# A chunked RWKV-7 chain of two products a chunk instead of three: the inverse times the keys and times the value terms is made once per group

## The chip, the cores and the metric

The kernel runs on one core of one Trainium2 chip. The metric is the device time of one execution, in microseconds (us). The core has five engines that run side by side, each with its own row of instructions taken in order: TensorE (PE, matrix products into PSUM), VectorE (DVE), ScalarE (ACT), GpSimd (POOL), and SyncE (SP), which here issues all DMA transfers. They wait for one another through semaphores.

## The reference

One decoder block on x (1 x 2048 x 1024), float32. After RMSNorm and an adaLN modulation, a single product with `w_in` gives the inputs of two token mixers and of their gates; a causal convolution branch and an RWKV-7 branch follow, are gated, projected and summed, and an output projection, the residual and a last RMSNorm close the block. The part that the change touches is the RWKV-7 recurrence of 16 heads of 64 channels:

```python
def step(state, inp):
    r_t, w_t, k_t, v_t, kk_t, b_t = inp
    sk = jnp.einsum('bhvk,bhk->bhv', state, kk_t)
    state = (state * w_t[:, :, None, :] - sk[..., None] * b_t[:, :, None, :]
             + v_t[..., None] * k_t[:, :, None, :])
    return state, jnp.einsum('bhvk,bhk->bhv', state, r_t)
...
kk = (k * k_k).astype(f32).reshape(hd)
kk = kk / jnp.maximum(jnp.sqrt(jnp.sum(kk * kk, axis=-1, keepdims=True)), L2_EPS)
...
o = _rwkv7_scan(r, decay.reshape(hd), k, v, kk, kk * a)
```

## The kernel before

**Tiling.** Four blocks of 512 tokens. In each block the input projection makes 73 tiles of 128 output channels x 512 tokens. Every such product is made of f32r matmuls of split operands (`h_hi,w_hi`, `h_lo,w_hi`, `h_hi,w_lo`), eight k-steps of three matmuls each, in the PSUM tile `ps_main`. These f32r rows are the bulk of PE's work. Each block has four groups of two pairs; a pair is two heads, 128 channels. Tokens are cut into chunks of 64, eight per block.

**The pair** (`pair`, line 720) prepares operands: decays `E1`, `E2`; `KR` (keys and receptances times decays) and `BK`; the products KR·BK masked into `As` (four quarters per chunk, the triangle to be inverted among them); `tk`, the transpose of BK; values `uv`. The squared norms `sq` are summed by eight matmuls with N=2 per pair into `rn`, which stays as a factor: it multiplies the triangles (`As<-As,rn`, two steps per pair) and, later, each chunk's solution.

**The group** (`group`, line 870) inverts 32 unit triangles of 64x64 (two pairs, two heads, eight chunks): the 32x32 diagonal parts on POOL over 31 steps (`La`, `TT`, reached by DMA through DRAM), the off-diagonal parts by 32x32 matmuls `lower` and `upper`. Then comes the chain over eight chunks with the state `S`, three products a chunk that each wait for the one before through DVE:

1. `xo<-S,KR` (state times keys); DVE adds the value term and writes `Xz`;
2. `xo<-Xz,As` (times the inverse; the next chunk's value term `xval` is interleaved, `xo<-uv,As`); DVE multiplies by `rn` and writes `uv`;
3. `xo<-uv,tk` (state increment, four products of one head each); four DVE steps write `S`.

After every second chunk eight more `xo<-uv,As` products give the outputs (`olast`). Behind the chain, outputs are normalised, transposed (`late<-ident,uv`), gated and stored.

**What sets the order.** In the first phase the program order is written by generators (`Task`) that a planner advances: `note` (line 85) keeps a modelled clock for each engine, and after each k-step (three f32r rows) tasks whose operands are ready on that clock may put their instructions, a burst, into the rows. `burst` lets a task wait up to `JOIN` for another burst while a chain runs. The order is fixed when the program is built; on the chip each engine takes its row in order. In the second phase (`pout`, `pmean`) a scheduler orders the rows. Every instruction is recorded at the helper's line 127, so names of tiles tell the places apart: `out<-in`.

Of the kernel before, what the change touches and what calls it, by code (L numbers as in the profile page):

```python
# [13 lines left out]
ALU = mybir.AluOpType  # L14
# [37 lines left out]
SEM, SWITCH, JOIN = 0.1, 0.14, 2.0  # L52
# [19 lines left out]
def hybrid_block(ctx: ExitStack, tc: tile.TileContext, x, vecs, convk, w2a2, final_g, ada, w_in, w_co, w_ro, w_o, crow, out,  # L72
# [436 lines left out]
    hones = bones.bitcast(F32)[:, 0::64]  # L509

    Xz = c1.tile([P, 2, 2, P], F32, name="Xz")
    nc.gpsimd.memset(Xz, 0.0)
# [207 lines left out]
    def pair(G, q_, box):  # L720
        b, pr, uv, Asb, rn = G.b, 2 * G.g + q_, G.uv, G.As[q_], G.rn
# [50 lines left out]
        pss = pa.tile([P, NCH // 2, 2], F32, name="aux", tag="aux")  # L772
# [30 lines left out]
        rlo = e1.tile([P, TB], F32R, name="s_lo", tag="s_lo")  # L803
# [16 lines left out]
        for e in range(2):  # L820
            sl = prow(e)
            tri = Asb[sl, :, e::2, kcol(e)]
            ENT[TRE].tensor_tensor(out=tri, in0=tri, in1=rq[sl].rearrange("p c h -> p h c").unsqueeze(3).broadcast_to(
                [64, 2, NCH // 2, CH]), op=ALU.mult)
# [31 lines left out]
    def opened(b, g, h, lora):  # L856
        G = Group()
        G.b, G.g, G.h, G.lora, G.tri, G.pairs, G.chained, G.gated, G.normed = b, g, h, lora, 0, 0, False, False, False
        G.uv = l3.tile([P, NCH, 2, P], F32, name="uv", tag="uv", bufs=2)
        for e in range(2):  # L860
            nc.gpsimd.memset(G.uv[prow(e), e::2], 0.0)
        G.As = [l3.tile([P, 2, NCH, P], F32, name="As", tag="As", bufs=ASB) for _ in range(2)]
        G.R = [{}, {}]
        G.rn = lt.tile([P, 2, NCH // 2, 2], F32, name="rn", tag="rn")
        return G
# [4 lines left out]
    def group(G, before):  # L870
        g, b, As, uv, rn, R = G.g, G.b, G.As, G.uv, G.rn, G.R
# [18 lines left out]
        nc.gpsimd.memset(TTf[0:64, 0::34], 1.0)  # L890
        nc.gpsimd.memset(TTf[64:128, 1::34], 1.0)
# [37 lines left out]
        yield both(ok(T11), free, bank("late"), bank("aux", 2))  # L929
# [16 lines left out]

        turns(lower)
# [4 lines left out]
        yield ok(Qs)  # L952

        turns(upper)
        with tc.high_priority(HP):
            for e in range(2):
                lo_, hi_ = quarters(e)
                for q in range(2):
                    nc.vector.tensor_copy(As[q][lo_, :, e::2, hi_], pq[e][lo_, q])
        locked[0] = False  # L960
        yield ok(*As)

        O = uv[:, 0::2]
        Sg = S[g]
# [3 lines left out]

        def xval(c, n):

            q, hh, hs = every[3 - n]
            nc.tensor.matmul(xo[c % 2][prow(c % 2), 2 + q, hs], As[q][:, hh, c, kcol(c % 2)], uv[:, c, q, hs],
                             start=(n == 0), stop=(n == 3), skip_group_check=True)

        def xcopy(c):
            nc.scalar.copy(Xz[prow(c % 2), c % 2], xo[c % 2][prow(c % 2), 2:4])

        def olast(c):
            for n, (q, hh, hs) in enumerate(every):
                for e in range(2):  # L980
                    nc.tensor.matmul(xo[e][vrow(e), q, hs], As[q][:, hh, c + e, rcol(e)], uv[:, c + e, q, hs],
                                     start=False, stop=(n == 3), skip_group_check=True)
            with tc.high_priority(HP):
                for e in range(2):
                    nc.scalar.copy(O[vrow(e), c // 2], xo[e][vrow(e), 0:2])

        yield bank("xo", 2)
        for n in range(4):
            xval(0, n)
        with tc.high_priority(HP):  # L990
            xcopy(0)
        for c in range(NCH):
            cc, e = c // 2, c % 2
            pr_, b_ = prow(e), xo[e]
            es = slice(e * 128, e * 128 + 128)
            Se = lt.tile([P, 2, P], F32, name="Se", tag="Se", bufs=1)
            for q in range(2):
                nc.tensor.matmul(b_[:, q, :], R[q]["KR"][:, cc, es], Sg[:, q, :], start=(q == 0), stop=False,
                                 skip_group_check=True)
            with tc.high_priority(HP):  # L1000
                for q in range(2):
                    nc.scalar.mul(Se[:, q, :], Sg[:, q, :], R[q]["pe"][:, c:c + 1])
                nc.vector.tensor_tensor(out=Xz[pr_, e], in0=b_[pr_, 0:2], in1=Xz[pr_, e], op=ALU.add)
            yield ok(Xz)

            for n, (q, hh, hs) in enumerate(every):
                nc.tensor.matmul(b_[pr_, q, hs], As[q][:, hh, c, kcol(e)], Xz[:, e, q, hs],
                                 start=(n == 0), stop=(n == 3), skip_group_check=True)
                if c + 1 < NCH:
                    xval(c + 1, n)  # L1010
            with tc.high_priority(HP):
                if c + 1 < NCH:
                    xcopy(c + 1)
                nc.vector.tensor_tensor(out=uv[pr_, c].rearrange("p q (h n) -> p q h n", n=64),
                                        in0=b_[pr_, 0:2].rearrange("p q (h n) -> p q h n", n=64),
                                        in1=rn[pr_, :, cc, :].unsqueeze(3).broadcast_to([64, 2, 2, 64]), op=ALU.mult)
            yield ok(uv)
            for q, hh, hs in every:
                nc.tensor.matmul(b_[hs, 2 + q, 0:64], R[q]["tk"][:, c, hs], uv[:, c, q, hs], start=False,
                                 stop=(q + hh == 2), skip_group_check=True)  # L1020
            with tc.high_priority(HP):
                for q, hh, hs in every:
                    nc.vector.scalar_tensor_tensor(out=Sg[hs, q, hs], in0=b_[hs, 2 + q, 0:64],
                                                   scalar=R[q]["pe"][hs, c:c + 1], in1=Se[hs, q, hs],
                                                   op0=ALU.mult, op1=ALU.add)
            yield ok(Sg)
            if e:
                olast(c - 1)
                yield ok(uv)
# [69 lines left out]
    def conv(b, h, j):  # L1099
# [21 lines left out]
        evac(value(project(h, ("in", T_VAL + j)), convs[-2:-1]))  # L1121
# [92 lines left out]
    def lora_split(ps, out_):  # L1214
        yield hx.room(3)
        lf, ll, lx = hx.take("lora"), hx.take("lora_lo"), hx.take("lora_x")
        yield from shifted(ps, T_LORA, lambda: lf)
        yield ok(lf)
# [439 lines left out]
```

## Time and profile before

| | |
|---|---|
| median of 3 runs | 2994.11 us (2994.05 to 2997.04) |
| profiled execution | 2994.35 us, span 2992.6 us |
| mean granted TensorE clock | 0.973 |
| ACT, POOL busy | 1064.4 us (36%), 1273.2 us (43%) |
| DMA | 680.02 MB, mean 227 GB/s |

A row of the timeline gives start, duration, engine, operation, and in brackets the idle time before it with what ended it. A row of the waits gives for whom an engine waited: total us, times, longest. A row of the groups gives busy us and mean ns of one. Matmuls are pipelined, so a recorded duration is longer than the distance to the next start; an f32 matmul leaves two records, a transpose or an f32r matmul one. The slices of the page show where PE is less than full: at the start, and otherwise in tenths:

```profile
PE   5999899989899999799999998999999997899998
DVE  6787787868677878685778686858597836543433
POOL 2464646532516565436356654354654624100000
```

The first phase ends near 2498 us (slice 34), and the output projection follows.

### The profile page before, as it was taken

What the parts mean: (1) busy time and instruction counts of PE and PEld (TensorE: products, weight loads), DVE (VectorE), ACT (ScalarE), POOL (GpSimd) and SP (SyncE); (2) the same over time, 40 slices, a digit from 0 to 9 for tenths busy, and PEclk for the clock granted to TensorE, in tenths of its full rate; (3) what the DMA queues carried; (4) which work ended last, traced back from release to release, by engine and by line L of the source; (5) the groups of instructions that cost most, each with busy time, mean ns of one, the idle gap of its engine ahead of it and who ended that gap; (6) DMA issues with size and microseconds to landing.
All of it is one profiled execution on the core that took longest, in us unless ns stands there. A gap on an engine that the chain in (4) does not pass through costs nothing. (4 is left out here: it accounts for less than half of the span.)

```text
span 2992.6 us, 51518 instructions
## 1 busy us (share of the span) xinstructions
PE 2793.2 (93%) x19152; PEld 2220.9 (74%) x19152; DVE 2055.5 (69%) x3671; ACT 1064.4 (36%) x2168; POOL 1273.2 (43%) x1793
## 2 busy tenths in 40 slices
PE   5999899989899999799999998999999997899998
PEld 4777777767677777577777775877777776788988
DVE  6787787868677878685778686858597836543433
ACT  4544343434233434333433344323334323221211
POOL 2464646532516565436356654354654624100000
PEclk9999999999999999899999998999999998999999
DMA  7785857666658576677677665765656857776665
GB/s 286 268 288 199 279 204 266 213 225 218 214 172 295 178 252 212 226 250 231 197 236 239 204 235 176 252 233 184 231 203 192 269 164 268 263 234 224 211 225 176
DMA packets 359051, 680.02 MB, mean 227 GB/s; under 512 B 131536, under 2 KB 150288, under 8 KB 358800
## 3 DMA queue, kind: packets, MB, share of 16 engines
q1 hardware_dynamic: 358800, 676.73, 67.1%
q8 instruction: 151, 2.47, 0.3%
q14 instruction: 100, 0.82, 0.1%
HBM read 494.08 MB, written 181.41 MB: 226 GB/s over the span
## 5 line engine op out<-in xcount | busy, mean ns | idle before, releaser
L127 PE MATMUL ps_main<-h_hi,w_hi 128*128 128x512 f32 x2432 | 1030.2, 424 | 25.0 <-ACT w_hi L127 11.8
L127 PE MATMUL ps_main<-h_hi,w_lo 128*128 128x512 f32 x2432 | 966.7, 397 | 21.4 <-POOL w_lo L127 13.0
L127 PE MATMUL ps_main<-h_lo,w_hi 128*128 128x512 f32 x2432 | 963.7, 396 | 3.2 <-issue 1.9
L127 DVE SCALAR_TENSOR_TENSOR acc<-u,ck,acc 128x512 f32<-128x512 f32 x928 | 699.2, 753 | 27.2
L127 PEld LDWEIGHTS ps_main<-h_hi,w_hi 128*128 128x128 f32 x2432 | 463.3, 191 | 135.1 <-ACT w_hi L127 13.1
L127 PEld LDWEIGHTS ps_main<-h_hi,w_lo 128*128 128x128 f32 x2432 | 462.7, 190 | 135.4 <-POOL w_lo L127 15.5
L127 PEld LDWEIGHTS ps_main<-h_lo,w_hi 128*128 128x128 f32 x2432 | 464.8, 191 | 83.4 <-DVE h_lo L127 3.2
L127 POOL TENSOR_TENSOR w_lo<-w_st,w_hi 128x1024 fp32r<-128x1024 f32 (+1 forms) x85 | 169.2, 1990 | 335.7 <-ACT w_hi L127 300.1
L127 POOL TENSOR_TENSOR itmp<-La,TT 128x126 f32<-128x126 f32 (+22 forms) x496 | 204.0, 411 | 82.4 <-DMA La<-dA 51.9
L127 ACT ACTIVATE th<-ps_main 128x512 f32<-128x512 f32 x160 | 95.5, 597 | 365.0 <-PE ps_main L127 318.2
L127 POOL TENSOR_TENSOR TT<-TT,itmp 128x126 f32<-128x126 f32 (+22 forms) x496 | 208.5, 420 | 38.9
L127 ACT CAST w_hi<-w_st 128x1024 fp32r<-128x1024 f32 (+1 forms) x135 | 127.5, 944 | 252.6 <-DMA w_st<-w_co_t 118.1
L127 DVE SCALAR_TENSOR_TENSOR S<-xo,pe,Se 64x64 f32<-64x64 f32 x512 | 145.1, 283 | 48.0 <-PE xo L127 35.0
L127 POOL TENSOR_TENSOR lny<-lny 128x512 f32<-128x512 f32 x90 | 118.0, 1318 | 125.4 <-DMA lny<-y_d 98.2
L127 PE MATMUL xo<-uv,As 128*64 128x64 f32 x2048 | 132.1, 229 | 0.6 <-DVE S L127 0.6
L127 PEld LDWEIGHTS xo<-uv,As 128*64 128x64 f32 x2048 | 105.3, 138 | 30.0 <-issue 26.1
L127 ACT COPY Xz<-xo 64x256 f32<-64x256 f32 x128 | 47.0, 367 | 204.8 <-PE xo L127 204.7
L127 DVE TENSOR_TENSOR As<-aux,maskA 128x512 f32<-128x512 f32 x128 | 82.3, 685 | 51.7 <-PE aux L127 51.4
L127 DVE TENSOR_TENSOR w_lo<-w_st,w_hi 128x1024 fp32r<-128x1024 f32 x50 | 66.2, 1324 | 68.6 <-PE ps_main L127 51.4
L127 ACT ACTIVATE Se<-S,pe 128x128 f32<-128x128 f32 x256 | 88.7, 394 | 66.9 <-DVE S L127 65.6
L127 DVE TENSOR_TENSOR uv<-xo,rn 64x256 f32<-64x256 f32 x128 | 54.0, 422 | 83.9 <-PE xo L127 83.1
L127 DVE TENSOR_TENSOR Xz<-xo,Xz 64x256 f32<-64x256 f32 x128 | 53.9, 421 | 79.8 <-PE xo L127 72.9
(286 smaller groups left out, 4908.9 us busy)
## 6 DMA issues: line engine op xcount, KB each, us to landing
w_hi<-kh_in SPq DMA_DIRECT2D x219, 512.0 KB, 4.2
w_lo<-kl_in SPq DMA_DIRECT2D x219, 512.0 KB, 5.4
w_st<-w_in_t SPq DMA_DIRECT2D x73, 512.0 KB, 4.8
kh_in<-w_hi SPq DMA_DIRECT2D x71, 512.0 KB, 4.7
kl_in<-w_lo SPq DMA_DIRECT2D x71, 512.0 KB, 3.8
lny<-y_d SPq DMA_DIRECT2D x72, 256.0 KB, 5.3
w_hi<-kh_ro SPq DMA_DIRECT2D x32, 512.0 KB, 4.3
w_lo<-kl_ro SPq DMA_DIRECT2D x32, 512.0 KB, 5.6
```

Source lines behind the costliest of these rows:

```text
L127: r = f(*a, **k)
```

## The change

Once per group, behind `lower`, 32 products of 64x64 (`values`) make each chunk's value term, which is copied into the unused half of `uv` (`keep64`). Behind `upper`, the keys are transposed by 16 products with the identity (`pk`), copied to `Kt`, multiplied by the inverse (`pw`, 32 products of 64x64) and written back into `KR`; 32 more (`solved`) multiply the value terms by the inverse. So each chunk needs two dependent products: `xo<-S,KR`, to which DVE adds the solved term and writes `uv`, and `xo<-uv,tk`. An even chunk's increment is made by two 128x128 products whose diagonal blocks are used; an odd chunk's increment and the two chunks' outputs are one burst. The norms: one f32 product with `bones` per pair sums `sq` into every row, one row per head goes to DRAM (`dN`), and the group loads them in the inverse's layout (`dn`); they set its diagonal (`TT`) and scale its rows (`La`). The `rn` factors and `Xz` are gone. The planner's prices for matmuls are new: parts of the array, rather than the kind of number, make a change cost. `u` gets three buffers, and the second half of the lora task is a task of its own.

PE, one even chunk of a chain in the second group, before (`xo` is the chain's PSUM tile; between the rows shown stand 3, 3 and 6 `ps_main` rows):

```order
L127 MATMUL xo<-S_441,KR 128x128 x2
...
L127 MATMUL xo<-Xz,As 64x64
L127 MATMUL xo<-uv,As 64x64
...
L127 MATMUL xo<-uv,tk 64x64 x4
...
L127 MATMUL xo<-S_441,KR 128x128 x2
```

The same place after, with the odd chunk too (6 `ps_main` rows in each gap):

```order
L129 MATMUL xo<-S_439,KR 128x128 x2
...
L129 MATMUL xo<-uv,tk 128x128 x2
...
L129 MATMUL xo<-S_439,KR 128x128 x2
...
L129 MATMUL xo<-uv,tk 64x64 x4
L129 MATMUL xo<-uv,As 64x64 x8
```

The product with `Xz` is gone, and the hops between the remaining two are six rows long, where they were three, three and six.

PE, from the end of the inverse to the chain in the same group, before (`As,Qs` is `upper`; 9 `ps_main` rows in the gap):

```order
L127 MATMUL late<-As,Qs 32x32
L127 MATMUL aux<-As,Qs 32x32
...
L127 MATMUL xo<-uv,As 64x64 x4
L127 MATMUL xo<-S_441,KR 128x128 x2
```

After (`ident,KR` is `pk`, `As,Kt` is `pw`, sixteen of each bank in turn, `uv,As` x32 is `solved`; gaps of 3 and 9 `ps_main` rows):

```order
L129 MATMUL aux<-As,Qs 32x32
L129 MATMUL xo<-ident,KR 64x128 x16
...
L129 MATMUL late<-As,Kt 64x64
L129 MATMUL aux<-As,Kt 64x64
...
L129 MATMUL xo<-uv,As 64x64 x32
...
L129 MATMUL xo<-S_439,KR 128x128 x2
```

The set-up of the chain has become two bursts of part-array products, 3 rows apart.

PE, the tail of a pair in the same group, before (gaps of 9, 6, 3 and 3 `ps_main` rows; `ident,BK` are the transposes into `tk`):

```order
L127 MATMUL aux<-KR,BK 128x128 x8
...
L127 MATMUL aux<-KR,BK 128x128 x8
...
L127 MATMUL aux<-ident,BK 128x128 x4
...
L127 MATMUL aux<-ident,BK 128x128 x4
L127 MATMUL aux<-rh,bones 128x512
L127 MATMUL aux<-s_lo,bones 128x512
...
L127 MATMUL aux<-ident,vv 128x128 x4
```

After (gaps of 6, 3 and 3):

```order
L129 MATMUL aux<-KR,BK 128x128 x8
...
L129 MATMUL aux<-KR,BK 128x128 x8
...
L129 MATMUL aux<-ident,BK 128x128 x8
L129 MATMUL aux<-rh,bones 128x512
L129 MATMUL aux<-s_lo,bones 128x512
...
L129 MATMUL aux<-ident,vv 128x128 x4
```

The bursts of the tail stand closer together, by three rows at each of the first two joints. At the first phase's end the last group's `late<-ident,uv` transposes stood behind the last `ps_main` row, eight in one burst; now four stand 36 and four 12 `ps_main` rows ahead of it, and `pmean` stands behind 97 `pout` rows instead of 22.

The diff, cut to its core:

```diff
@@ note
-        t = max([now[0], vt.get(name, 0.0), used.get(k_, 0.0)] + [ready.get(key(a), 0.0) + SEM for a in ins])
+        t = max([now[0], vt.get(name, 0.0), used.get(k_, 0.0) if name != "PE" or k_[:2] != "xo" else 0.0] + [ready.get(key(a), 0.0) + SEM for a in ins])
@@
-                kd, c = F32, 0.107
+                part, c = False, 0.218
             else:
-                kd, (K_, M_), N_ = ins[1].dtype, (ins[0].shape[0], size(ins[0])), size(ins[1])
-                c = 0.015 + N_ / 2400 if kd == F32R else 2 * max(0.107 * M_ / 128, N_ / 1200) * (
-                    0.55 if K_ <= 64 else 0.75 if M_ <= 64 else 1.0)
-            if kd != kind[0]:
-                kind[0], c = kd, c + SWITCH
+                K_, M_, N_ = ins[0].shape[0], size(ins[0]), size(ins[1])
+                part = K_ <= 64 or M_ <= 64
+                c = N_ / 600 * ((0.27 if K_ <= 64 else 0.54) if M_ <= 64 else 0.89 if part else 1.0)
+                if ins[1].dtype == F32R:
+                    part, c = False, 0.015 + N_ / 2400
+            if part != kind[0]:
+                kind[0], c = part, c + (0.1 if part else 0.24)
@@ pair
-        for c in range(NCH):
-            nc.tensor.matmul(pss[prow(c % 2), c // 2, :], sq[:, c * CH:c * CH + CH], hones, start=True, stop=True,
-                             skip_group_check=True)
-        rq = rn[:, q_]
-        nc.vector.tensor_scalar(out=rq, in0=pss, scalar1=L2_EPS * L2_EPS, scalar2=-1.0, op0=ALU.max, op1=ALU.mult)
-        nc.vector.reciprocal(rq, rq)
+        nc.tensor.matmul(pss, bones.bitcast(F32), sq, start=True, stop=True)
+        ssr = e1.tile([P, TB], F32, name="ssr", tag="sq")
+        nc.scalar.copy(ssr, pss)
+        yield ok(ssr)
+        for hh in range(2):
+            nc.sync.dma_start(G.dN[q_, hh:hh + 1].rearrange("o c e k t -> o (c e k t)"), ssr[64 * hh:64 * hh + 1])
@@
-            ENT[TRE].tensor_tensor(out=tri, in0=tri, in1=rq[sl]...)
@@ group
+        dn = lt.tile([P, 32], F32, name="dn", tag="dn")
+        for half in range(2):
+            nc.sync.dma_start(dn[64 * half:64 * half + 64], G.dN.rearrange("q h c e k t -> (q h c e k) t"))
+        yield ok(dn)
+        nc.vector.tensor_scalar(out=dn, in0=dn, scalar1=L2_EPS * L2_EPS, scalar2=-1.0, op0=ALU.max, op1=ALU.mult)
+        nc.vector.reciprocal(dn, dn)
...
+            nc.gpsimd.tensor_copy(TTf[sl, half::34], dn[sl, half::2])
+        yield ok(La)
+        nc.vector.tensor_tensor(out=La, in0=La, in1=dn.unsqueeze(1).broadcast_to([P, 32, 32]), op=ALU.mult)
@@
+        def rows64(bank_, mul):
+            for turn in range(2):
+                for cl in range(2):
+                    for q in range(2):
+                        for hh in range(2):
+                            for e in range(2):
+                                n_ = turn ^ e
+                                mul(e, 2 * n_ + cl, q, hh, bank_[n_][prow(e), cl, q, 64 * hh:64 * hh + 64], ...)
+
+        def keep64(bank_, half):
+            for e in range(2):
+                (nc.scalar.copy if e else nc.vector.tensor_copy)(uv[prow(e), 4 * half + e:4 * half + 4:2], bank_[half][prow(e)])
+
+        def values(e, cc, q, hh, dst, kw):
+            vr, c, hs = vrow(e), 2 * cc + e, slice(64 * hh, 64 * hh + 64)
+            nc.tensor.matmul(dst, As[q][vr, hh, c, kcol(e)], uv[vr, c, q, hs], **kw)
+
+        def solved(e, cc, q, hh, dst, kw):
+            pr_, c, hs = prow(e), 2 * cc + e, slice(64 * hh, 64 * hh + 64)
+            nc.tensor.matmul(dst, As[q][pr_, hh, c, kcol(e)], uv[pr_, c, q, hs], **kw)
 
         turns(lower)
...
+        xv = two()
+        rows64(xv, values)
+        for half in range(2):
+            keep64(xv, half)
+        yield ok(Qs, uv)
 
         turns(upper)
...
+                    nc.tensor.matmul(pk[q][prow(e), cc, :], R[q]["KR"][:, cc, CH * (1 + e):CH * (2 + e)], ident, ...)
+            nc.scalar.copy(Kt[:, q], pk[q])
+        yield ok(Kt, *As)
...
+                nc.tensor.matmul(pw[e][hs, q, cc, :], Kt[prow(e), q, cc, hs], As[q][prow(e), hh, 2 * cc + e, kcol(e)], ...)
...
+                    nc.scalar.copy(R[q]["KR"][:, :, CH * (1 + e):CH * (2 + e)], pw[e][:, q])
+        xu = two()
+        rows64(xu, solved)
+        for half in range(2):
+            keep64(xu, half)
@@ the chain
-                nc.vector.tensor_tensor(out=Xz[pr_, e], in0=b_[pr_, 0:2], in1=Xz[pr_, e], op=ALU.add)
-            yield ok(Xz)
-
-            for n, (q, hh, hs) in enumerate(every):
-                nc.tensor.matmul(b_[pr_, q, hs], As[q][:, hh, c, kcol(e)], Xz[:, e, q, hs], ...)
-                if c + 1 < NCH:
-                    xval(c + 1, n)
...
-                nc.vector.tensor_tensor(out=uv[pr_, c]..., in0=b_[pr_, 0:2]..., in1=rn[pr_, :, cc, :]..., op=ALU.mult)
+                nc.vector.tensor_tensor(out=uv[pr_, c], in0=b_[pr_, 0:2], in1=uv[pr_, c], op=ALU.add)
             yield ok(uv)
...
+            if e == 0:
+                for q in range(2):
+                    nc.tensor.matmul(b_[:, 2 + q, :], R[q]["tk"][:, c, :], uv[:, c, q, :], start=False, stop=(q == 1), ...)
@@ conv
-            u = e2.tile([P, HALO + TB], F32, name="u", tag="u")
+            u = e2.tile([P, HALO + TB], F32, name="u", tag="u", bufs=3)
@@ lora
+        Task(lora_parts(lf, ll, lx, out_), 0)
```

More of the change, by code (lines that the diff above doesn't have):

```diff
@@ L507, in hybrid_block @@
         nc.vector.tensor_scalar(out=wlo[:, i, :], in0=ident, scalar1=0.0, scalar2=None, op0=ALU.mult)
-    hones = bones.bitcast(F32)[:, 0::64]
-    Xz = c1.tile([P, 2, 2, P], F32, name="Xz")
-    nc.gpsimd.memset(Xz, 0.0)
     one1 = c1.tile([P, 1], F32, name="one1")
@@ L819, in pair @@
                     in0=pA[hh], in1=flat(maskA).unsqueeze(1).broadcast_to([P, 2, 256]), op=ALU.mult)
[L820 to L824, printed above, removed]
         G.tri += 1
@@ L859, in opened @@
         G.uv = l3.tile([P, NCH, 2, P], F32, name="uv", tag="uv", bufs=2)
-        for e in range(2):
-            nc.gpsimd.memset(G.uv[prow(e), e::2], 0.0)
+        G.dN = dp.tile([2, 2, NCH // 2, 2, 2, 32], F32, name="dN", tag="dN", bufs=3)
         G.As = [l3.tile([P, 2, NCH, P], F32, name="As", tag="As", bufs=ASB) for _ in range(2)]
         G.R = [{}, {}]
-        G.rn = lt.tile([P, 2, NCH // 2, 2], F32, name="rn", tag="rn")
         return G
@@ L928, in group @@
                 nc.vector.transpose(heads(T11[:, q])[lo_], heads(As[q])[lo_, e::2, lo_])
-        yield both(ok(T11), free, bank("late"), bank("aux", 2))
+        yield both(ok(T11, uv), free, bank("late"), bank("aux", 2), bank("xo", 2))
         locked[0] = True
@@ L945, in upper, with two @@
             nc.tensor.matmul(pq[e][lo_, q, hh, c, :], Qs[hi_, q, hh, c, :], As[q][hi_, hh, 2 * c + e, hi_], **kw)
+        O = uv[:, 0::2]
+        Sg = S[g]
+        def two():
+            return [px.tile([P, 2, 2, P], F32, name="xo", tag="xo") for _ in range(2)]
+        def rows64(bank_, mul):
[5 more added lines that the diff above has]
+                                n_ = turn ^ e
+                                mul(e, 2 * n_ + cl, q, hh, bank_[n_][prow(e), cl, q, 64 * hh:64 * hh + 64],
+                                    dict(start=(cl + q + hh == 0), stop=(cl + q + hh == 3), skip_group_check=True))
+        def keep64(bank_, half):
[7 more added lines that the diff above has]
+            nc.tensor.matmul(dst, As[q][pr_, hh, c, kcol(e)], uv[pr_, c, q, hs], **kw)
         turns(lower)
@@ L959, in group @@
                     nc.vector.tensor_copy(As[q][lo_, :, e::2, hi_], pq[e][lo_, q])
+        Kt = lt.tile([P, 2, NCH // 2, P], F32, name="Kt", tag="La", bufs=1)
+        pk = [px.tile([P, NCH // 2, P], F32, name="xo", tag="xo") for _ in range(2)]
+        for q in range(2):
+            for cc in range(NCH // 2):
+                for e in range(2):
+                    nc.tensor.matmul(pk[q][prow(e), cc, :], R[q]["KR"][:, cc, CH * (1 + e):CH * (2 + e)], ident,
+                                     start=(cc == 0), stop=(cc == NCH // 2 - 1), skip_group_check=True)
+            nc.scalar.copy(Kt[:, q], pk[q])
@@ new lines, in group @@
+        yield ok(Kt, *As)
+        pw = [p_.tile([P, 2, NCH // 2, CH], F32, name=n_, tag=n_) for p_, n_ in ((pl, "late"), (pa, "aux"))]
+        for n, (q, hh, cc) in enumerate(every):
+            hs = slice(64 * hh, 64 * hh + 64)
+            for e in range(2):
+                nc.tensor.matmul(pw[e][hs, q, cc, :], Kt[prow(e), q, cc, hs], As[q][prow(e), hh, 2 * cc + e, kcol(e)],
+                                 start=(q + cc == 0), stop=(q == 1 and cc == NCH // 2 - 1), skip_group_check=True)
@@ L960, in group @@
+        with tc.high_priority(HP):
+            for q in range(2):
+                for e in range(2):
+                    nc.scalar.copy(R[q]["KR"][:, :, CH * (1 + e):CH * (2 + e)], pw[e][:, q])
+        xu = two()
+        rows64(xu, solved)
+        for half in range(2):
+            keep64(xu, half)
         locked[0] = False
-        yield ok(*As)
-        O = uv[:, 0::2]
-        Sg = S[g]
+        yield ok(uv, R[0]["KR"], R[1]["KR"])
         xo = [px.tile([P, 4, P], F32, name="xo", tag="xo") for _ in range(2)]
@@ L967, in group @@
         every = [(q, hh, slice(64 * hh, 64 * hh + 64)) for q in range(2) for hh in range(2)]
[L969 to L978, printed above, removed]
-            for n, (q, hh, hs) in enumerate(every):
[L980 to L991, printed above, removed]
         for c in range(NCH):
@@ L1011, in group @@
[L1011 to L1016, printed above, removed]
-            yield ok(uv)
-            for q, hh, hs in every:
-                nc.tensor.matmul(b_[hs, 2 + q, 0:64], R[q]["tk"][:, c, hs], uv[:, c, q, hs], start=False,
-                                 stop=(q + hh == 2), skip_group_check=True)
+                nc.vector.tensor_tensor(out=uv[pr_, c], in0=b_[pr_, 0:2], in1=uv[pr_, c], op=ALU.add)
@@ new lines, in group @@
+            yield ok(uv)
+            if e == 0:
+                for q in range(2):
+                    nc.tensor.matmul(b_[:, 2 + q, :], R[q]["tk"][:, c, :], uv[:, c, q, :], start=False, stop=(q == 1),
+                                     skip_group_check=True)
+            else:
+                for q, hh, hs in every:
+                    nc.tensor.matmul(b_[hs, 2 + q, 0:64], R[q]["tk"][:, c, hs], uv[:, c, q, hs], start=False,
+                                     stop=(q + hh == 2), skip_group_check=True)
@@ L1027, in group @@
             if e:
-                olast(c - 1)
-                yield ok(uv)
+                for n, (q, hh, hs) in enumerate(every):
+                    for i in range(2):
+                        nc.tensor.matmul(xo[i][vrow(i), q, hs], As[q][:, hh, c - 1 + i, rcol(i)], uv[:, c - 1 + i, q, hs],
+                                         start=False, stop=(n == 3), skip_group_check=True)
+                with tc.high_priority(HP):
+                    for i in range(2):
+                        nc.scalar.copy(O[vrow(i), cc], xo[i][vrow(i), 0:2])
@@ L1030, in group @@
+            yield ok(Sg, uv)
         G.chained = True
```

24 lines of the change are left out of this document (10 added, 14 removed).

## The prediction

> **What bounds the kernel now.** I read the page's busy shares first, then the waits of TensorE (PE), then its timeline through one chunk chain, and last the groups of the engines that feed the chain. Times are against the profiled execution: 2994.35 us, of which 1.75 us lie outside its span; the median of the runs is 0.24 us lower, so a difference in one is a difference in the other.
>
> ```profile
> span 2992.6 us, 51518 instructions
> PE 2793.2 (93%) x19152; PEld 2220.9 (74%) x19152; DVE 2055.5 (69%) x3671; ACT 1064.4 (36%) x2168; POOL 1273.2 (43%) x1793
> ```
>
> PE is busy for 93% of the span, 24 points more than the next engine. It issues in order: what a change adds to PE's row of work is paid, and what it adds elsewhere is paid only where PE comes to wait. The waits (total us, times, longest):
>
> ```profile
> PE late L127 <- DVE T L127: 27.8, 7, 13.0
> PE aux L127 <- POOL KR L127: 14.4, 12, 4.0
> PE pmean L127 <- POOL ys L127: 12.9, 1, 12.9
> PE xo L127 <- ACT Xz L127: 7.3, 16, 0.5
> PE xo L127 <- DVE uv L127: 2.0, 2, 1.5
> ```
>
> The chain's own operands (`uv`, `Xz`) make PE wait 9.3 us in all; the projection's f32r matmuls between the hops fill the rest. So a shorter chain by itself is worth next to nothing, and the question is what the changed set of small f32 matmuls ("bursts" between f32r rows) costs PE. The timeline of PE (start, duration) prices them:
>
> ```profile
> 1108.40 0.40 PE L127 MATMUL ps_main<-h_hi,w_lo 128*128 128x512 f32 x1
> 1108.72 0.68 PE L127 MATMUL xo<-uv,As 128*64 128x64 f32 x8
> 1109.86 0.71 PE L127 MATMUL xo<-S,KR 128*128 128x128 f32 x4 [0.46 <-ACT Xz L127]
> ...
> 1110.64 0.40 PE L127 MATMUL ps_main<-h_lo,w_hi 128*128 128x512 f32 x1
> ...
> 1112.39 0.39 PE L127 MATMUL ps_main<-h_hi,w_lo 128*128 128x512 f32 x1
> 1112.71 0.45 PE L127 MATMUL xo<-uv,tk 128*64 128x64 f32 x8
> ...
> 1113.43 0.40 PE L127 MATMUL ps_main<-h_lo,w_hi 128*128 128x512 f32 x1
> 1113.67 0.39 PE L127 MATMUL ps_main<-h_hi,w_lo 128*128 128x512 f32 x1
> ...
> 1114.36 0.39 PE L127 MATMUL ps_main<-h_hi,w_lo 128*128 128x512 f32 x1
> 1114.59 0.61 PE L127 MATMUL xo<-S,KR 128*128 128x128 f32 x4
> ...
> 1115.27 0.40 PE L127 MATMUL ps_main<-h_lo,w_hi 128*128 128x512 f32 x1
> ...
> 1118.99 0.40 PE L127 MATMUL ps_main<-h_hi,w_lo 128*128 128x512 f32 x1
> 1119.32 0.69 PE L127 MATMUL xo<-uv,As 128*64 128x64 f32 x16
> ...
> 1120.27 0.40 PE L127 MATMUL ps_main<-h_lo,w_hi 128*128 128x512 f32 x1
> ```
>
> Durations overlap, so a burst is priced by starts. From 1113.67 to 1114.36 are three f32r intervals, 0.23 us each. A burst costs the time from the last f32r start before it to the second f32r start behind it, less two intervals (0.46): S·KR 0.45, four `uv,tk` 0.58, eight `uv,As` 0.82. An f32 matmul leaves two records, so x8 is four matmuls. Four more 128x64 matmuls cost 0.24, or 0.06 each, and what is left, 0.34, is the price of going from full-array to part-array matmuls and back. S·KR uses the full array and carries no such price: 0.225 for a 128x128.
>
> **The change on PE.** The other prices by the same rule:
>
> ```profile
> 943.37 0.40 PE L127 MATMUL ps_main<-h_hi,w_lo 128*128 128x512 f32 x1
> 943.70 0.63 PE L127 MATMUL aux<-bones,sq 128*64 128x2 f32 x16
> ...
> 944.60 0.40 PE L127 MATMUL ps_main<-h_lo,w_hi 128*128 128x512 f32 x1
> 1095.06 0.39 PE L127 MATMUL ps_main<-h_hi,w_lo 128*128 128x512 f32 x1
> 1095.37 1.16 PE L127 MATMUL aux<-KR,BK 64*128 64x128 f32 x16
> ...
> 1096.81 0.40 PE L127 MATMUL ps_main<-h_lo,w_hi 128*128 128x512 f32 x1
> ...
> 1097.97 1.03 PE L127 MATMUL aux<-ident,BK 128*128 128x128 f32 x8
> ...
> 1099.54 0.39 PE L127 MATMUL aux<-rh,bones 128*128 128x512 f32 x1
> 1101.60 0.40 PE L127 MATMUL ps_main<-h_hi,w_lo 128*128 128x512 f32 x1
> 1101.93 0.21 PE L127 MATMUL late<-T,As 32*32 32x32 f32 x1
> ...
> 1103.40 0.39 PE L127 MATMUL ps_main<-h_lo,w_hi 128*128 128x512 f32 x1
> ```
>
> The eight N=2 norms cost 0.77 (0.43 without the 0.34); eight KR·BK 1.29, so 0.12 each, about half of a 128x128 since two row halves run side by side; thirty-two 32x32 1.34, so 0.031 each.
>
> 1. Matmul time. 128x64 products go from 2048 to 768 (the `Xz` product and its neighbour, and the even chunks' `tk`): −1280 × 0.06 = −77. 128 products `uv,tk` of 128x128 come: +128 × 0.225 = +29. Norms: 32 pairs, 0.43 gives way to a 512-column f32 product, four times 0.225 = 0.90: +15. Transposing keys: 256 products of 128x64 with N=128, twice the columns of an 0.06 one: +256 × 0.12 = +31. The 64x64 products (`values`, `pw`, `solved`: 96 per group, 1536) have no row. Bounds: 0.031 (the 32x32, half the columns) and 0.12 (no overlap). In them successive matmuls take opposite row halves and different PSUM banks, as KR·BK and the 32x32 do, whose rows show two at a time; for N=64 that is half of 0.12, 0.06: +92 (bounds +48, +184). Sum +90.
>
> 2. Part-array changes. Per group before: 16 (`Xz`, `tk` of eight chunks), 4 for the last outputs, 1 at the start, 4 + 2 in the pairs (KR·BK, norms), 2 in the inverse; 29 × 16 = 464, and 440 in PE's order, where some stand side by side. After: 4 per group (odd `tk` and outputs together), 3 in the set-up, 4 for KR·BK, 173 in the order. −267 × 0.34 = −91. There are 19 more changes between two part shapes; at half that price, +3.
>
> 3. The chain's start. `uv,As`, S·KR and its wait cost 2.24 − 0.46 = 1.78; the parts are 0.34 + 0.24 + 0.45 = 1.03. The 0.75 left, mostly the wait on `Xz`, happens 16 times and goes: −12. What is late next there is the KR copy behind `pw`; nine f32r rows (2.1 us) cover it.
>
> 4. The hops. After, six f32r rows (1.4 us) lie between S·KR and `tk`, and six between `tk` and S·KR. DVE's work there:
>
> ```profile
> L127 DVE TENSOR_TENSOR uv<-xo,rn 64x256 f32<-64x256 f32 x128 | 54.0, 422 | 83.9 <-PE xo L127 83.1
> L127 DVE SCALAR_TENSOR_TENSOR S<-xo,pe,Se 64x64 f32<-64x64 f32 x512 | 145.1, 283 | 48.0 <-PE xo L127 35.0 <-ACT w_hi L127 0.9 <-ACT M L127 0.6
> L127 DVE TENSOR_TENSOR As<-As,rn 64x512 f32<-64x512 f32 x64 | 51.9, 810 | 1.8
> L127 DVE SCALAR_TENSOR_TENSOR acc<-u,ck,acc 128x512 f32<-128x512 f32 x928 | 699.2, 753 | 27.2
> L127 DVE TENSOR_TENSOR As<-aux,maskA 128x512 f32<-128x512 f32 x128 | 82.3, 685 | 51.7 <-PE aux L127 51.4
> L127 ACT COPY tk<-aux 128x512 f32<-128x512 f32 x64 | 34.7, 591 | 64.9 <-PE aux L127 64.9
> ```
>
> The add (0.42) fits into 1.4. The four S operations are 1.13 and meet 1.4 too, tightly; the second S·KR matmul needs only the last two. I take 0, with +0.2 × 128 = +26 as the upper end if DVE is held by an `acc` step. The set-up's `Kt` copy has three rows (0.7) for about 0.6 and a start: 16 × 0.2 = +3.
>
> 5. The pair's tail is moved. Before, six f32r rows stood between the second KR·BK and the transposes, and three between transposes and `rh`; after, three and none (24 pairs at least). KR·BK began at 1095.37, its mask steps (2 × 0.685) free both banks about 2.5 us later; transposes will start 0.7 earlier than the 1097.97 shown, a 0.1 wait. `rh` needs a bank: four transposes (the columns of four 0.225 / 2, as they leave one record, not two) take 0.45, their tail 0.2 (a recorded matmul outlasts its interval: 0.39 against 0.23), the copy 0.59: 1.24 from the transposes' start, against 0.9 for all eight: 0.3. Sum 0.4 × 30 = +12. The first KR·BK gets six more rows (36 instead of 30), which covers most of the 12 waits on POOL's KR (mean 1.2): −8.
>
> 6. The norm path and the inverse. Two DMA writes per pair (64 issues on SP) and two loads per group (32) ride with the inverse's own transfers. DVE loses two 0.81 steps ahead of the inverse and gains one 128x1024 product, by its size some 1.2 us; POOL's diagonal copy replaces its memset. Per group between −1.6 and +2.5 us, felt only at the 7 waits on `T`: −11 to +18, taken as 0, as most groups have slack there. DVE's other sums (the 128 `rn` steps become the `uv` add, the `Xz` add and `As` product go, 64 copies come) lower its load; ACT and SP have room. The third `u` buffer and the lora split only let gates run earlier: 0.
>
> 7. The phase boundary.
>
> ```profile
> 2498.68 0.67 PE late L127 x4
> ...
> 2522.61 20.87 PE pout L127 x170
> ```
>
> Before, the last group's output transposes stand behind all f32r rows, and `pmean` behind 22 `pout` rows. After, the transposes stand 36 and 12 f32r rows ahead of the end and `pmean` behind 97 `pout` rows, 75 × 0.123 = 9.2 us later, which is work done inside the 12.9 us wait. −9 (bounds 0 and −16).
>
> Sum: +90 −91 +3 −12 +3 +12 −8 −9 = −12, with 0 for the rest; 2994 − 12 = 2982 us. The first two terms nearly cancel, so the sign hangs on the small ones.
>
> **The rivals.**
>
> A. The 64x64 products do not run side by side. Each costs 0.12: +92 more, 3074 us; from 0.072 each the change is slower. Against it: both row-split kinds in the trace do overlap. For it: 128x64 weights are new for every matmul here, and none of the rows has K and M of 64.
>
> The Trainium skill, "TensorEngine Tiling (Array Packing)", Gotcha 1, asks that different row tiles write to different PSUM banks; the new loops alternate banks for each row half, so by that rule A does not happen, and the 0.12 of KR·BK, which writes two banks in turn, agrees.
>
> B. The pair's tail costs more than 0.4. DVE and ACT serve their queues in order; an `acc` step (0.753) ahead of each mask step and a cast ahead of the copy (0.591) would add up to 2.1 us per pair, 67 in all; half of that, +34 over the forecast, gives 3016. It decides from 18 us, 0.56 per pair. For it: DVE is 69% busy, most of it with `acc`; against it: mask steps now wait for PE (51.4 us), not for DVE.
>
> C. Four 64x64 products at a time, 0.031 each: −44, 2938. The order speaks against it: in each run of them only one row half with one column half alternates with the other, and the sixteen 32x32 places are also filled by twos.
>
> The Trainium skill, same page, Tiling Modes, lists four independent 64x64 tiles, and sixteen of 32x32; by it C is possible where all four are fed, and the 0.031 of the 32x32 in this trace shows only two at a time.
>
> D. Nothing measurable: the inverse starts later by up to 2.5 us at the seven waits (+18) or S comes late (+26 at most), and this eats the small gains: 2994 within 6 us.
>
> E. The chain's shortening pays by itself: excluded beyond the 9.3 us of waits on `uv` and `Xz`, already in the sum.
>
> **How the numbers follow.** 0.2%, 6 us, is about what a measurement can tell from no change. Forecast (some 6 to 30 us faster, 2964 to 2988) 0.46; C 0.06; D 0.14; B and tight S hops together 0.2; A 0.14. Faster 0.52, same 0.14, slower 0.34. A range that leaves out C and A (0.20) goes from 2955 to 3025: the low end takes the lower bounds of terms 6 and 7 (−11, −7) and some of 3, the high end B at its middle with a part of D.
>
> **What would show it.** Groups `xo<-uv,As`, `aux<-As,Kt` starting 0.06 apart in the timeline (term 1; 0.12 is A, 0.031 C); bursts `S,KR` and `uv,tk` 128x128 at 0.45 (term 2); no wait on `Xz` and S·KR with less than 0.1 of idle before it (3, 4); `aux <- ACT tk` and `aux <- DVE As` in the waits near 12 us in sum and `POOL KR` near 6 (5; 40 or more is B); `late <- DVE T` near 28 (6; 45 is D); `pmean` near 4 (7). The forecast is wrong if PE's waits in all grow by over 20 us, or the 64x64 price is off by over 0.01 (15 us).

## The result

The changed kernel takes 3078.12 us (median of 4 runs, 3068.1 to 3080.61), the kernel before 2995.57 us beside it: 1.0264 of before, 95% interval 1.0235 to 1.0293. The forecast was 2982 us, range 2955 to 3025. The ratio is that of the mean times, and by it the change costs some 79 us. None of the rivals names the cause, although rival A's 3074 us lies next to the measured time.

### The profile page after: what moved, and what is told of

Its sections match the earlier page's. It is cut to its first block, busy times and chain, and to the rows that moved or that the text cites. A ratio compares the mean times of both kernels' runs of the same rounds, so it can differ in the third digit from the quotient of the medians.

```text
span 3066.4 us, 53344 instructions
## 1 busy us (share of the span) xinstructions
PE 2807.9 (92%) x19984; PEld 2287.7 (75%) x19984; DVE 2029.4 (66%) x3525; ACT 1111.8 (36%) x2232; POOL 1264.2 (41%) x1762
## 4 chain that ended last, share of the span: by engine, by line
PE 39%; DVE 9%; POOL 8%; DMA 7%; issue 3%; SPq 1%; ACT 1%; DVEq 0%; POOLq 0%; ACTq 0%
PE ps_main L129 25%; PE xo L129 5%; PE pout L129 5%; POOL TT L129 2%; PE aux L129 2%; POOL itmp L129 2%; DVE acc L129 2%; DVE S L129 2%; PE late L129 2%; SPq L129 1%; POOL lny L129 1%; DMA dn<-dN 1%; DMA zb<-bv_d 1%; POOL oc L129 1%; DMA w_st<-w_ro_t 1%
## 5 line engine op out<-in xcount | busy, mean ns | idle before, releaser
L129 PE MATMUL ps_main<-h_hi,w_hi 128*128 128x512 f32 x2432 | 1017.4, 418 | 24.0 <-ACT w_hi L129 9.4
L129 POOL TENSOR_TENSOR w_lo<-w_st,w_hi 128x1024 fp32r<-128x1024 f32 (+1 forms) x87 | 176.4, 2027 | 364.1 <-ACT w_hi L129 337.7
L129 PE MATMUL xo<-uv,As 64*64 64x64 f32 (+1 forms) x3072 | 132.5, 226 | 94.6 <-DVE S L129 93.6
L129 ACT COPY uv<-xo 64x256 f32<-64x256 f32 (+1 forms) x192 | 84.3, 439 | 343.8 <-PE xo L129 197.8
L129 PEld LDWEIGHTS xo<-uv,As 64*64 64x64 f32 (+1 forms) x3072 | 113.6, 139 | 104.2 <-DVE S L129 102.4
L129 DVE TENSOR_TENSOR uv<-xo,uv 64x256 f32<-64x256 f32 x128 | 54.0, 422 | 120.9 <-PE xo L129 118.1
L129 PEld LDWEIGHTS aux<-KR,BK 64*128 64x128 f32 x1024 | 65.7, 191 | 46.3 <-POOL KR L129 23.1
```

The source lines that it names most:

```text
L129: r = f(*a, **k)
```

## The profile after

The profiled execution took 3068.1 us, its span 3066.4 us. The page's head, then the waits of PE:

```profile
span 3066.4 us, 53344 instructions
PE 2807.9 (92%) x19984; PEld 2287.7 (75%) x19984; DVE 2029.4 (66%) x3525; ACT 1111.8 (36%) x2232; POOL 1264.2 (41%) x1762
```

```profile
PE xo L129 <- DVE S L129: 94.8, 65, 3.5
...
PE aux L129 <- POOL KR L129: 15.1, 14, 3.6
PE late L129 <- DVE T L129: 13.8, 5, 6.0
...
PE aux L129 <- DVE As L129: 10.4, 6, 4.0
...
PE aux L129 <- ACT tk L129: 3.9, 8, 2.2
...
PE pmean L129 <- POOL ys L129: 0.3, 1, 0.3
```

PE's idle time has grown from 2992.6 − 2793.2 = 199 to 3066.4 − 2807.9 = 259 us. One row alone holds more than the whole difference: `xo` waits 94.8 us for DVE's `S` steps, 65 times; there are 64 odd chunks. In the kernel before, the same row reads:

```profile
PE xo L127 <- DVE S L127: 0.6, 1, 0.6
```

In PE's timeline the place is the odd chunk's burst, increment and outputs together:

```profile
1134.27 0.39 PE L129 MATMUL ps_main<-h_hi,w_lo 128*128 128x512 f32 x1
1134.59 0.45 PE L129 MATMUL xo<-uv,tk 128*64 128x64 f32 x8
1134.87 0.28 PE L129 MATMUL xo<-uv,As 128*64 128x64 f32 x2
1136.44 0.68 PE L129 MATMUL xo<-uv,As 128*64 128x64 f32 x14 [1.29 <-DVE S L129]
...
1137.39 0.40 PE L129 MATMUL ps_main<-h_lo,w_hi 128*128 128x512 f32 x1
```

And DVE's row over the same time:

```profile
1135.16 1.23 DVE L129 SCALAR_TENSOR_TENSOR S<-xo,pe,Se 64x64 f32<-64x64 f32 x4 [0.53 <-PE xo L129]
```

One output product (two records) goes through, into the even chunk's bank. The second is for the odd chunk's bank, from which the four `S` steps read the increment; it starts at 1136.44, just behind their end at 1136.39. By the prediction's rule the burst costs 3.12 − 0.46 = 2.66 us, where 0.34 + 12 × 0.06 = 1.06 was reckoned. The outputs read `uv` and `As`, both ready before the burst begins, and write other columns of the tile than the steps read. The wait is one that the program asks for: in the trace the instruction at 1136.44 carries a semaphore wait, which the profile lays to DVE. In the kernel before, the outputs also came behind the `S` steps, but in most chunks six f32r rows lay in between, and PE did not wait:

```profile
1117.34 0.45 PE L127 MATMUL xo<-uv,tk 128*64 128x64 f32 x8
...
1119.32 0.69 PE L127 MATMUL xo<-uv,As 128*64 128x64 f32 x16
```

The terms of the forecast can be read from the same trace. The set-up of the chain:

```profile
1119.17 0.40 PE L129 MATMUL ps_main<-h_hi,w_lo 128*128 128x512 f32 x1
...
1120.63 1.97 PE L129 MATMUL xo<-ident,KR 128*64 128x128 f32 x32
...
1122.87 0.39 PE L129 MATMUL ps_main<-h_lo,w_hi 128*128 128x512 f32 x1
1123.10 0.40 PE L129 MATMUL ps_main<-h_hi,w_lo 128*128 128x512 f32 x1
1123.42 0.27 PE L129 MATMUL late<-As,Kt 64*64 64x64 f32 x1
...
1124.82 2.03 PE L129 MATMUL xo<-uv,As 64*64 64x64 f32 x63
...
1127.12 0.39 PE L129 MATMUL ps_main<-h_lo,w_hi 128*128 128x512 f32 x1
...
1128.74 0.40 PE L129 MATMUL ps_main<-h_hi,w_lo 128*128 128x512 f32 x1
1128.97 0.61 PE L129 MATMUL xo<-S,KR 128*128 128x128 f32 x4
...
1129.65 0.39 PE L129 MATMUL ps_main<-h_lo,w_hi 128*128 128x512 f32 x1
```

`pw` and `solved` cost 4.02 − 0.46 = 3.56 us; less 0.34 these are 64 products at 0.050 us. The burst with `pk` costs 3.24; less 0.34 and 32 of 0.031 these are 16 at 0.12. The first S·KR costs 0.45, with no wait.

## Experiments

Ratios are of mean times, to the kernel before, run beside each on the same chip.

**Outputs first.** In an odd chunk the eight output products stand ahead of the increment, in the same burst; the copy of the outputs stays behind both:

```diff
+            if e:
+                for n, (q, hh, hs) in enumerate(every):
+                    for i in range(2):
+                        nc.tensor.matmul(xo[i][vrow(i), q, hs], As[q][:, hh, c - 1 + i, rcol(i)], uv[:, c - 1 + i, q, hs], ...)
             if e == 0:
...
                 for q, hh, hs in every:
                     nc.tensor.matmul(b_[hs, 2 + q, 0:64], R[q]["tk"][:, c, hs], uv[:, c, q, hs], ...)
...
             if e:
-                for n, (q, hh, hs) in enumerate(every):
-                    for i in range(2):
-                        nc.tensor.matmul(xo[i][vrow(i), q, hs], As[q][:, hh, c - 1 + i, rcol(i)], uv[:, c - 1 + i, q, hs], ...)
```

> The changed kernel with one edit: in an odd chunk the eight output products stand ahead of the four `uv,tk` products in the same burst, so no output product has to wait for the four DVE steps that read the increments. Wait theory (the changed kernel is slow because the output products wait 64 times about 1.46 us for DVE's `S` steps, 94.8 us in its waits): that wait falls under 10 us, the burst from 2.66 to about 1.2 us, and the time from 3078 to 2985 us (2975 to 2995), below the kernel before. Price theory (rival A: the 64x64 products take twice what was reckoned): no change, 3078. Planner theory (the new matmul prices put rows in worse places): no change beyond 10 us, 3068 to 3088.

Measured: 2968.96 us, 0.9927 (0.9906 to 0.9948). The waits and one burst:

```profile
PE xo L129 <- DVE S L129: 1.2, 3, 0.8
```

```profile
993.06 0.40 PE L129 MATMUL ps_main<-h_hi,w_lo 128*128 128x512 f32 x1
993.39 0.69 PE L129 MATMUL xo<-uv,As 128*64 128x64 f32 x16
993.90 0.40 PE L129 MATMUL xo<-uv,tk 128*64 128x64 f32 x8
...
994.58 0.40 PE L129 MATMUL ps_main<-h_lo,w_hi 128*128 128x512 f32 x1
```

The wait is gone, the burst costs 1.52 − 0.46 = 1.06 us, and 3.4% of the time goes with it. The same instructions in another order are faster than the kernel before. The price theory and the planner theory, which both gave about 3078, fall as causes of the loss.

**Outputs in a burst of their own.**

```diff
             if e:
+                yield ok(Sg)
                 for n, (q, hh, hs) in enumerate(every):
```

> The changed kernel with one edit: the outputs are a burst of their own again, which the planner places after `S` is ready on its clock, six f32r rows behind `uv,tk`. Wait theory: the 94.8 us go, 64 more changes into and out of the part array come at 0.34 us (+22): 3006 us (2995 to 3020). Price theory: only the +22: 3100. Planner theory: 3085 to 3105.

Measured: 2988.32 us, 0.9991 (0.9973 to 1.0009). Of the three theories only the wait theory gives so short a time, and it was 18 us too high: the time lies below its range. The join, without its wait, makes 0.9991 − 0.9927 = 0.0064 or 19 us between the two versions, where 64 × 0.34 = 22 was reckoned. That match is partly luck, since the two also differ by 9.5 us in a wait at the phase boundary, here and with the outputs first:

```profile
PE pmean L129 <- POOL ys L129: 13.8, 1, 13.8
PE pmean L129 <- POOL ys L129: 4.3, 1, 4.3
```

The price of a join is better read from the bursts: 0.58 and 0.82 us apart (in the prediction), 1.06 together, so 0.34 less.

**The join alone, in the kernel before.**

```diff
-            yield ok(Sg)
             if e:
                 olast(c - 1)
-                yield ok(uv)
+            yield ok(Sg, uv)
```

> The kernel before with this one part of the change alone: the outputs stand right behind an odd chunk's `uv,tk`, in one burst. Wait theory: 64 waits of about 1.46 us come (+94), 64 array changes go (-22): 2995 + 72 = 3067 us (3050 to 3075). Price and planner theories: only the array changes go: 2973 us.

Measured: 3040.4 us, 1.0181 (1.0148 to 1.0214); the sign is the wait theory's, the size is below its range. The waits:

```profile
PE xo L127 <- DVE S L127: 84.4, 65, 3.7
...
PE pmean L127 <- POOL ys L127: 3.8, 1, 3.8
```

The wait is 10 us shorter than reckoned, and `pmean` waits 9 us less than in the kernel before: 84 − 22 − 9 = 53, against 50 between the medians. Other waits moved too, so this is a rough account. But this one part brings the wait, and a loss of 50 us, without any of the new products.

**One row half after the other.** The loops of `rows64` with e outermost, so that successive products use the same quarter of the array:

```diff
-            for turn in range(2):
-                for cl in range(2):
-                    for q in range(2):
-                        for hh in range(2):
-                            for e in range(2):
-                                n_ = turn ^ e
+            for e in range(2):
+                for turn in range(2):
+                    for cl in range(2):
+                        for q in range(2):
+                            for hh in range(2):
+                                n_ = turn
```

> The changed kernel with the products `values` and `solved` (1024 of 64x64) issued first all for one row half, then all for the other, so that successive products use the same quarter of the array. If they run side by side in the changed kernel (its bursts give 0.05 to 0.06 us each), each now takes about 0.12: +55 to +70 us, the burst `pw` + `solved` from 3.56 to about 5.3 us. If they did not run side by side there (price theory), nothing changes. The wait on `S` stays as it is in both.

Measured, one execution: 3132.01 us, 64 us above the changed kernel's profiled execution. `pw` (unchanged) and `solved` in PE's timeline:

```profile
1153.29 0.40 PE L129 MATMUL ps_main<-h_hi,w_lo 128*128 128x512 f32 x1
...
1155.01 3.71 PE L129 MATMUL xo<-uv,As 64*64 64x64 f32 x64
...
1159.00 0.40 PE L129 MATMUL ps_main<-h_lo,w_hi 128*128 128x512 f32 x1
```

The burst grows from 3.56 to 5.71 − 0.46 = 5.25 us: 32 products cost 0.053 more each, which is 0.10 in place of 0.050; 1024 of them make 54 of the 64 us. One at a time would be about 0.11, by the 0.225 of a full product with twice the columns. So in the changed kernel they run two at a time, and rival A is excluded.

**The odd increment in a tile of its own.**

```diff
-            yield ok(uv)
+            yield both(ok(uv), bank("late")) if e else ok(uv)
+            if e:
+                own = pl.tile([P, 2, P], F32, name="late", tag="late")
...
-                    nc.tensor.matmul(b_[hs, 2 + q, 0:64], R[q]["tk"][:, c, hs], uv[:, c, q, hs], start=False, ...)
+                    nc.tensor.matmul(own[hs, q, 0:64], R[q]["tk"][:, c, hs], uv[:, c, q, hs], start=(q == 0), ...)
```

> The changed kernel, outputs behind `uv,tk` as in it, but an odd chunk's increment goes into the PSUM tile `late` instead of the chain's tile `xo`, into which the outputs are written. If the outputs wait for the `S` steps because both use one tile (the steps read it, the outputs write other columns of it), the wait on `S` falls from 94.8 to under 10 us and the time to that of the outputs placed first, 0.993 of the kernel before, give or take 0.006 for the borrowed bank. If it is the join itself or another operand that makes them wait, the wait stays and the time is 1.02 to 1.03 of before.

Measured: 2975.79 us, 0.9939 (0.9919 to 0.9959).

```profile
PE xo L129 <- DVE S L129: 2.7, 3, 1.0
```

```profile
1125.32 0.40 PE L129 MATMUL ps_main<-h_hi,w_lo 128*128 128x512 f32 x1
1125.64 0.45 PE L129 MATMUL late<-uv,tk 128*64 128x64 f32 x8
1125.92 0.64 PE L129 MATMUL xo<-uv,As 128*64 128x64 f32 x16
...
1126.83 0.40 PE L129 MATMUL ps_main<-h_lo,w_hi 128*128 128x512 f32 x1
```

The order is that of the changed kernel, the outputs directly behind the increment, and they do not wait: the burst costs 1.51 − 0.46 = 1.05 us. So neither the join nor an operand makes them wait, but the common tile: in this program a product that writes one part of it waits until DVE has read another part. What the chip would do without that wait was not tried.

The Trainium skill, "PSUM — Partial Sum Buffer", section "PSUM bank collisions raise a hardware error", says that two engines may not use one bank and the same 32 partitions of it at once, and that the chip does not stall but reports an error. By that rule the wait is necessary here, since the steps read all 128 partitions of the odd chunk's bank while outputs would write half of them; that the wait goes with another bank agrees, and no run here shows a collision.

**The planner's new prices alone**, in the kernel before (`note` as in the diff, all else as before).

> The kernel before with the planner's new matmul prices alone. By the terms of the forecast that the prices bring about (pair's tail +12, KR and boundary -8 and -9) it is 5 us faster, 0.998 of before, 0.994 to 1.002. If the planner's prices are where the changed kernel lost time (planner theory), 1.01 or more. If they are where the repaired kernel gains, 0.993.

Measured: 2993.11 us, 1.0000 (0.9988 to 1.0012). They neither cost nor gain there.

**Outputs first, with the old prices** (`note` as before).

> The changed kernel with outputs first and the planner's old prices. If the prices are worth little: 0.990 to 0.997, as with the new ones (0.9927). If the gain of that kernel came from the prices: 0.999 to 1.003.

Measured: 2975.22 us, 0.9939 (0.9924 to 0.9955); with the new prices 0.9927. The gain does not come from the new prices.

**Outputs first in the kernel before.** Three products a chunk as before, the outputs ahead of an odd chunk's increment in one burst.

> The kernel before, three products a chunk as it was, with the outputs joined to an odd chunk's `uv,tk` and placed first. 64 changes into and out of the part array go: -22 us, 0.9927 of before. If that is so, the join is worth as much as the whole change, and making the keys and values once per group gains nothing beyond it; if it stays above 0.996, the shorter chain's own saving is what shows in the repaired kernel.

Measured: 2980.86 us, 0.9960 (0.9946 to 0.9974), at the edge of the second expectation: of the 0.73% of the changed kernel with outputs first, a good half comes with the join and its order alone.

That leaves 0.33%, 10 us, for the rest of the change, and this remainder is not safely shown. The two ratios come from different chips, and their intervals touch. On one chip and with the same old prices, the three-product kernel takes 2980.86 us and the two-product kernel 2975.22 us. The clocks granted to TensorE differ as well: 0.973 to 0.977 in the runs of the first, 0.978 to 0.984 in those of the second. Among the runs of the kernel before on that chip, 0.973 goes with 2994 to 3002 us and the one run at 0.979 with 2986 us, so a clock higher by 0.005 may be worth the whole 5.6 us. Whether the two-product chain gains anything beyond the join stays open, and so does whether the change itself brings the higher clock.

**Prices from the trace.** Outputs first, and in `note` first a transpose at 0.111 us:

```diff
-                part, c = False, 0.218
+                part, c = False, 0.111
```

> Outputs first, and the planner's price of a transpose at 0.111 us, as the trace has it, instead of 0.218. In 9 of 32 pairs three f32r rows come back between the transposes and `rh`, where PE now waits about 0.6 us for ACT's copy of `tk`. If the tail's wait is net time: -5 us, 0.991 of before. If stalls only move when the planner's prices change: 0.9927 within 0.002.

Measured: 2960.21 us, 0.9883 (0.9865 to 0.9900). Then also the part-array products near the trace's prices:

```diff
-                c = N_ / 600 * ((0.27 if K_ <= 64 else 0.54) if M_ <= 64 else 0.89 if part else 1.0)
+                c = N_ / 600 * ((0.5 if K_ <= 64 else 0.54) if M_ <= 64 else 0.56 if part else 1.0)
```

> Outputs first with all f32 prices of the planner near those of the trace (transposes 0.111, KR and BK 0.12, 64x64 0.053, 32x32 0.027 each). If better prices make better places: 0.988 to 0.991. If stalls only move: 0.9927 within 0.002.

Measured: 2955.96 us, 0.9869 (0.9852 to 0.9886), the fastest version tried, 39 us below the kernel before. A pair's tail in it, which in the changed kernel stood without f32r rows:

```profile
1086.93 0.66 PE L129 MATMUL aux<-ident,BK 128*128 128x128 f32 x4
1087.34 0.48 PE L129 MATMUL ps_main<-h_hi,w_hi 128*128 128x512 f32 x1
...
1088.13 0.60 PE L129 MATMUL aux<-ident,BK 128*128 128x128 f32 x4
1088.48 0.47 PE L129 MATMUL aux<-rh,bones 128*128 128x512 f32 x1
1088.80 0.39 PE L129 MATMUL aux<-s_lo,bones 128*128 128x512 f32 x1
```

Three f32r rows stand between the two halves of the transposes, and `rh` follows without a wait. Both versions are faster than either of their expectations, and the theory that stalls only move was wrong here. The first expectation counted on rows coming back in 9 of 32 pairs; in its trace they stand between the transposes, or between them and `rh`, in 29 pairs, and in 30 in the second version, against none with outputs first alone. There, `rh` came about 0.44 us late in 28 pairs (worked out for one pair below), some 12 us, which is of the size of the gain.

Why better prices gain 0.4 to 0.6% here, by ratios from different chips, is still not settled. With the old prices the rows stand in 28 pairs as well, and that version was no faster (0.9939 against 0.9927). In the kernel before, the change's prices leave the rows in only one pair, and the time stays the same. The trace's prices were not tried there.

## Why the prediction was wrong

The step that failed is term 2, where "4 per group (odd `tk` and outputs together)" was counted as array changes saved and nothing else, together with term 4, which followed the hops and did not ask what an output product waits for when it stands directly behind `tk`. That adjacency brought 94.8 us of waits, more than the loss of 79 us; removing it by order alone (0.9927) or removing the wait by another tile (0.9939) turns the loss into a gain, and adding it to the kernel before costs 1.8%. The prediction's own sign of being wrong, waits of PE that grow by over 20 us, is there: its idle time grew by 59 us. None of the rivals had the cause, and the range, up to 3025, had no room for it.

A hint was in the diff. `note` no longer lets a PE write into `xo` wait for the tile's readers, so the planner's clock did not see the cost of this join. That line did not make the join, which the chain's own code fixes by having no pause between increment and outputs; together with the new prices the line was tried in the kernel before and cost nothing.

The rule of the Trainium skill cited at the run with the odd increment in its own tile could have pointed to the wait: it speaks of banks and partitions, not of columns, and the forecast did not hold the joined burst against it.

The other steps, by their own numbers:

1. Matmul time: `pk` 0.12 as reckoned; 64x64 at 0.050 against 0.06, 15 us better over 1536. Right in kind.
2. Array changes without the wait: 0.34 a join by the bursts, as reckoned; the 19 us between two versions, against 22, hold other waits. Right for the join; the other changes saved were not measured apart.
3. The chain's start: the wait on `Xz` is gone and S·KR costs 0.45. Right.
4. Hops: PE's waits on `xo` for DVE beside the join were near nothing (`S` 1.2 us in all once the outputs stand first). Right.
5. The pair's tail. In the trace of the changed kernel:

```profile
1108.88 1.25 PE L129 MATMUL aux<-ident,BK 128*128 128x128 f32 x8
1110.21 0.50 PE L129 MATMUL aux<-rh,bones 128*128 128x512 f32 x1
```

1.33 from transposes to `rh`, less 0.89 of transposes, is a wait of 0.44; 0.4 was reckoned. Twenty-nine of the 32 pairs have this form. The view of the waits shows little of it, because the recorded transposes last until 0.08 us before `rh`. Rival B's 40 us or more in the waits did not come: `As` and `tk` 14.3 us. But `POOL KR` waits stayed (15.1 against 14.4), so the −8 was wrong: six more rows ahead of the first KR·BK did not shorten them.
6. The inverse: `late` waits for `T` 13.8 us against 27.8, within the bounds (−11 to +18) but for 3 us; rival D's +18 did not come.
7. The phase boundary: `pmean` waits 0.3 us instead of 12.9, and the split version, where it waits 13.8, shows that this gain hangs on where the last rows fall. The −9 was right there, and the position is fragile.

So the sum without the join's wait was near: −12 reckoned, −22 (0.9927 of 2994) measured with the outputs first. How near is partly luck: the 64x64 products alone came out 15 us better, and the runs with outputs first had a granted clock of 0.977 to 0.981, those of the kernel before beside them 0.973 to 0.978. Rival A gave a time close to the measured one by a mechanism that the 0.050 us and the one-half run exclude: a matching total proves no mechanism.

The rule of the Trainium skill, "TensorEngine Tiling (Array Packing)", Gotcha 1, by which rival A should not happen, agrees with the 0.050 us of the alternating order. The 0.10 us of the other order does not test it, since only one row half is in use at a time there, and no run here alternates two row halves on one bank.

## What to carry to other kernels

When two bursts are joined, ask of each instruction in the joined burst not only what it reads but which tile it writes and who still reads that tile; a wait that six rows of other work had covered is paid in full after the join. Where the order is free, put first what nothing waits behind, here the outputs, so that the same join costs nothing. A planner that is told such a write is free can't show its cost. Planner prices taken from the trace brought 0.4 to 0.6% here, by a way that is only partly known.

## What the runs showed that was not expected

In this program a product waits for a reader of other columns of its PSUM tile, about 1.5 us each time (94.8 us over 65 waits), and hardly at all with the reader's data in another tile (2.7 us). A 64x64 product cost 0.050 us alternating between row halves and 0.10 us with one half only, so a pair of quarters gave a factor of two.
